# Spreading RMS-norm factors over the partitions: two transposes in place of a matmul with ones

## The chip, the cores and the metric

The kernel runs on one core of a Trainium2 chip. The metric is the device time of one execution in microseconds. The kernel before was timed three times: 938.61, 938.96 and 939.32 us, median 938.96.

## The reference, cut to what matters

The reference is a two-layer streaming encoder on 256 tokens of 1024 features, float32. Each layer is a half-step SwiGLU feed-forward block (FFN), a mixer, and a second half-step FFN. The mixer of layer 0 is a recurrent block (causal convolution and a gated linear recurrence), that of layer 1 differential attention with shared keys and values. Every block starts with an RMS norm over the features:

```
y = x * rsqrt(mean(x*x, axis=-1) + 1e-6) * g
FFN:  x = x + 0.5 * ((silu(h @ w_gate) * (h @ w_up)) @ w_down)      h = rmsnorm(x, g), hidden width 2816
```

The factor rsqrt(...) is one number per token. It commutes with the matrix product, so it can be applied to the product in place of the input.

## The kernel before, in words

The residual x stays in SBUF with the features on the partitions: eight tiles x[d] of 128 x 256 (tokens along the free axis). A block's input is g * x, split into a high part and a low part in fp32r; the weights are split in the same way, piece by piece, by ScalarE (whi) and VectorE (wlo) as they arrive in DMAs of 1 MB. A product of an FFN is made of two matmuls for each 128 x 128 weight block (mm2): whi against both parts of the input, 512 columns, and wlo against the high part, 256 columns. Elsewhere it is three matmuls of 256 columns (mm3), and in the projections of the attention three of 512.

In an FFN (ffn) the gate and up products of two f-blocks are interleaved first (FG = 2, 64 matmuls), then come f-blocks 2 to 21 (640 matmuls), then eight down products (352 matmuls; in the last FFN one of the eight goes by mm3). After the opening two f-blocks the factors are asked for (rb_fn), and finish scales each f-block: the two parts of the sum leave PSUM without the factor, and one VectorE product per f-block applies rb to gate and up together.

The factors come from rstd. While a block writes x[d], sumsq adds its squares into acc. rstd then makes two products of acc with a column of ones, tokens on the partitions (each is two instructions in the profile), VectorE scales and shifts them (rv), and GpSimd raises to the power -1/2 (rt, 128 x 2: the factor of token p and of token 128 + p). For the FFNs and the recurrent block the factors are needed along the free axis, the same on every partition: VectorE multiplies the identity by each column of rt into a diagonal matrix (diag), TensorE multiplies ones with it (two instructions in the profile), and ScalarE copies the 128 x 256 result to SBUF (rb). This happens five times: in the four FFNs, numbered 0 to 3 here (names f10, f20, l1, f21), and in the recurrent block (mix0). The attention's norm (mix1) takes rt alone (bcast=False).

The order of the work is not that of the program text. Every operation is recorded with its costs (cost, lines 121 to 165), then Recorder.plan lays out a list schedule: at each step it takes the engine that can start first, and there, among the operations that can start within HOLD = 60 ns of the first one, that with the longest tail of work behind it; the tail of a TensorE operation counts all of TensorE's operations that follow in the program text. HOP = 94 is added between engines. The costs that matter here, in the planner's ns: a transpose 109 with a latency of 220; an fp32r matmul 0.4428 per column + 3.3; an fp32 matmul of one column 222 with a latency of 392, of 256 columns 430; a VectorE addition of 256 columns 335, rv 70 with a latency of 156; the power 640 with a latency of 680. The plan then is emitted in that order, so that on the chip each engine runs a fixed list. All instructions go through one line of the emitting loop, so the profile has them all as L378; they are told apart by the names of their tiles: aux is the PSUM pool of two banks that rstd uses, mm the other six banks, w the scratch tiles (diag among them), xs, b and xk inputs of matmuls.

Of the kernel before, what the change touches and what calls it, by code (L numbers as in the profile page):

```python
# [11 lines left out]
F32 = mybir.dt.float32  # L12
# [3 lines left out]
ALU = mybir.AluOpType  # L16
AX = mybir.AxisListType

P = 128
D = 1024  # L20
KD = 8
T = 256
# [393 lines left out]
def trunk(ctx: ExitStack, tc, plan, xT, wts, vec, rows, eye, out):  # L416
    nc = Recorder(tc.nc)

    def pool(name, bufs, **kw):
        return Pool(nc, ctx.enter_context(tc.tile_pool(name=name, bufs=bufs, **kw)), bufs, plan and plan[1])  # L420
# [7 lines left out]
    psa = pool("psa", AB, space=bass.MemoryType.PSUM)  # L428
# [5 lines left out]
    ident = const.tile([P, P], F32, name="ident")  # L434
    ones = const.tile([P, P], F32, name="ones")
# [112 lines left out]
    def rstd(name, bcast=True):  # L548
        acc = acc_state["t"]
        ps = psa.tile([P, 512], F32, name="aux")  # L550
        for t in range(NT):
            nc.tensor.matmul(out=ps[:, t:t + 1], lhsT=acc[:, t * P:(t + 1) * P], rhs=ones[:, 0:1],
                             start=True, stop=True)
        v = wk.tile([P, NT], F32, name="rv")
        nc.vector.tensor_scalar(v, ps[:, 0:NT], 1.0 / D, EPS, op0=ALU.mult, op1=ALU.add)
        rt = const.tile([P, NT], F32, name=f"rt_{name}")
        nc.gpsimd.tensor_tensor(out=rt, in0=v, in1=mhalf[:, 0:NT], op=ALU.pow)
        if not bcast:
            return rt, None
        diag = w1()  # L560
        for t in range(NT):
            nc.vector.tensor_scalar(diag[:, t * P:(t + 1) * P], ident, rt[:, t:t + 1], None, op0=ALU.mult)
        pb = psa.tile([P, 512], F32, name="aux")
        nc.tensor.matmul(out=pb[:, 0:T], lhsT=ones, rhs=diag, start=True, stop=True)
        rb = wk.tile([P, T], F32, name="rb")
        nc.scalar.copy(out=rb, in_=pb[:, 0:T])
        return rt, rb
# [10 lines left out]
    def w1(shape=(P, T), dt=F32):  # L578
        return wk.tile(list(shape), dt, name="w1", bufs=10)
# [170 lines left out]

    xs_mix = new_xs()
    ffn(0, xs, lambda: rstd("f10"), prep(xs_mix, V_MIX[0]), small)

    def recurrent(xs, rb_fn, after):
# [102 lines left out]

    xs_f20 = new_xs()
    recurrent(xs_mix, lambda: rstd("mix0"), prep(xs_f20, V_F2[0]))

    xs_f11 = new_xs()
# [3 lines left out]
    def after_l0(d):  # L865
        pr1(d)
        split_scaled(xkv[d], x[d], vt[:, V_KV + d:V_KV + d + 1])

    ffn(1, xs_f20, lambda: rstd("f20"), after_l0)

    kvrt = {}
# [287 lines left out]
```

## Time and profile before

| | |
|---|---|
| median of three runs | 938.96 us |
| the profiled execution | 939.56 us |
| its span, first to last instruction | 937.5 us |
| outside the span | 2.06 us |
| granted TensorE clock | 0.999 of full speed |
| DMA queue that loads the weights | 51.8% of 16 engines |

The engines in the rows are PE (TensorE's matmuls), PEld (its weight loads), DVE (VectorE), ACT (ScalarE), POOL (GpSimd). A row of the timeline or of a group reads out<-in: for a matmul the moving operand comes first, then the stationary one. A matmul's record runs until its result is written, so the records of successive matmuls overlap; what one costs is the distance from its start to that of the next. The chain of waits is followed back from the last instruction, so a stretch on PE in it means that nothing else held PE up there.

### The profile page before, as it was taken

The page shows a single profiled execution, that of the slowest core. Times are in us where ns is not written, and L with a number is a line of the kernel's source. Part 1 is how long each engine was busy: PE and PEld are TensorE (multiplying, and loading weights), DVE is VectorE, ACT ScalarE, POOL GpSimd, SP SyncE. Part 2 cuts the span into 40 slices and gives each one's busy share as a digit, 9 for nine tenths or more (in the row PEclk, how much of TensorE's full clock was granted, in tenths as well). Part 3 has the DMA queues.
Part 4 walks back from the last instruction along what each step waited for, and adds up shares of the span by engine and source line. Part 5 has one row for each costly group of instructions (what it writes and reads, how often), then busy time and mean ns, then how long its engine had stood idle before and what let it go on. Part 6 is the DMA issues. An engine that isn't in the chain of part 4 may idle for free.

```text
span 937.5 us, 14663 instructions
## 1 busy us (share of the span) xinstructions
PE 930.3 (99%) x5586; PEld 823.8 (88%) x5586; DVE 723.0 (77%) x1226; ACT 579.0 (62%) x1039; POOL 31.1 (3%) x42
## 2 busy tenths in 40 slices
PE   8999999999999999999999999999999999999998
PEld 6888888899998888888888888888878988888887
DVE  7898777679898878867688887666987688888651
ACT  7665565559976565655556566554589866565541
POOL 0210000000000000000000000001230000000000
PEclk9999999999999999999999999999999999999999
DMA  8755555553365555555545555555443545555540
GB/s 310 255 184 196 195 184 197 198 189 135 136 225 186 204 194 180 182 200 200 182 180 182 195 202 185 181 189 191 159 138 133 180 172 187 180 186 203 203 157 17
DMA packets 25990, 172.31 MB, mean 184 GB/s; under 512 B 3136, under 2 KB 4288, under 8 KB 5568
## 3 DMA queue, kind: packets, MB, share of 16 engines
q1 hardware_dynamic: 25920, 171.39, 51.8%
q8 instruction: 43, 0.70, 0.3%
q14 instruction: 27, 0.22, 0.1%
HBM read 170.33 MB, written 1.05 MB: 183 GB/s over the span
## 4 chain that ended last, share of the span: by engine, by line
PE 94%; DVE 3%; POOL 1%; DMA 1%; issue 0%; ACT 0%; SPq 0%; ACTq 0%
PE mm L378 92%; PE aux L378 2%; DVE w L378 1%; DVE wlo L378 1%; DMA xa<-xT 1%; DVE ss L378 0%; POOL facq L378 0%; POOL fac L378 0%; POOL rt_mix L378 0%; ACT w L378 0%; SPq L378 0%; ACT whi L378 0%; ACT xs L378 0%; DVE fac L378 0%; DVE xa L378 0%
## 5 line engine op out<-in xcount | busy, mean ns | idle before, releaser
L378 PE MATMUL mm<-xs,whi 128*128 128x512 f32 (+1 forms) x1632 | 532.5, 379 | 2.1 <-DVE xs L378 1.2
L378 DVE TENSOR_TENSOR wlo<-raw,whi 128x1024 fp32r<-128x1024 f32 (+1 forms) x321 | 390.9, 1220 | 130.5 <-ACT whi L378 129.8
L378 ACT CAST whi<-raw 128x1024 fp32r<-128x1024 f32 (+1 forms) x321 | 335.5, 1048 | 203.2 <-PE mm L378 184.1
L378 PE MATMUL mm<-xs,wlo 128*128 128x256 f32 x1520 | 425.9, 281 | 0.1
L378 PEld LDWEIGHTS mm<-xs,whi 128*128 128x128 f32 x1632 | 298.4, 188 | 62.5 <-DVE xs L378 1.5
L378 PE MATMUL mm<-b,whi 128*128 128x512 f32 (+1 forms) x982 | 293.4, 360 | 0.0
L378 PEld LDWEIGHTS mm<-xs,wlo 128*128 128x128 f32 x1520 | 287.1, 189 | 0.8 <-DVE wlo L378 0.5
L378 PE MATMUL mm<-b,wlo 128*128 128x256 f32 x832 | 233.2, 281 | 0.0
L378 PEld LDWEIGHTS mm<-b,whi 128*128 128x128 f32 x982 | 174.8, 189 | 29.6 <-issue 0.3
L378 PEld LDWEIGHTS mm<-b,wlo 128*128 128x128 f32 x832 | 157.5, 189 | 0.0
L378 ACT ACTIVATE w<-mm 128x256 f32<-128x256 f32 x207 | 79.5, 385 | 117.2 <-PE mm L378 112.4
L378 DVE TENSOR_TENSOR w<-mm,w 128x256 f32<-128x256 f32 x176 | 73.5, 421 | 28.4 <-ACT w L378 27.9
L378 DVE TENSOR_TENSOR w<-w,rb 128x512 f32<-128x512 f32 x88 | 60.1, 686 | 0.4
L378 DVE TENSOR_TENSOR w<-w,w 128x256 f32<-128x256 f32 (+2 forms) x104 | 45.2, 439 | 0.3 <-ACT w L378 0.3
L378 PE MATMUL mm<-whi,xk 128*128 128x512 f32 x128 | 41.2, 396 | 0.0
L378 ACT ACTIVATE w<-w 128x256 f32<-128x256 f32 x88 | 36.4, 417 | 2.4 <-DVE w L378 2.2
L378 DVE TENSOR_TENSOR b<-w,b 128x256 fp32r<-128x256 f32 x88 | 36.4, 416 | 1.9 <-ACT b L378 1.9
L378 ACT CAST b<-w 128x256 fp32r<-128x256 f32 x88 | 35.4, 406 | 2.9 <-DVE w L378 2.8
L378 DVE SCALAR_TENSOR_TENSOR xa<-mm,xa 128x256 f32<-128x256 f32 x32 | 13.5, 423 | 27.1 <-PE mm L378 18.9
L378 PEld LDWEIGHTS mm<-whi,xk 128*128 128x128 f32 x128 | 23.8, 188 | 4.6
L378 PE MATMUL mm<-wlo,xk 128*128 128x512 f32 x64 | 25.1, 393 | 0.0
L378 ACT ACTIVATE xs<-xa,vt 128x256 fp32r<-128x256 f32 x40 | 19.5, 502 | 7.3 <-DVE xa L378 7.3
(124 smaller groups left out, 485.3 us busy)
## 6 DMA issues: line engine op xcount, KB each, us to landing
raw<-wts SPq DMA_DIRECT2D x159, 1024.0 KB, 4.8
raw<-wts SPq DMA_DIRECT2D x3, 512.0 KB, 7.5
outT<-xa SPq DMA_DIRECT2D x8, 128.0 KB, 2.0
xa<-xT SPq DMA_DIRECT2D x3, 256.0 KB, 6.6
raw<-wts SPq DMA_DIRECT2D x2, 256.0 KB, 4.4
rw<-rows SPq DMA_DIRECT2D x1, 320.0 KB, 5.0
xa<-xT SPq DMA_DIRECT2D x1, 260.0 KB, 3.8
ident<-eye SPq DMA_DIRECT2D x1, 64.0 KB, 9.2
```

Source lines behind the costliest of these rows:

```text
L378: getattr(getattr(self.nc, op.eng), op.fn)(*op.a, **op.k)
```

## The change

The two scalings of the identity and the product with ones go. In their place are two transposes on TensorE. Each takes one column of rt, read with a step of zero so that the 128 x 1 column stands for a 128 x 128 matrix with equal columns; its transpose has the factors along the free axis on every partition. The copy to rb is the same. The planner runs anew on the changed list of operations.

```diff
         nc.gpsimd.tensor_tensor(out=rt, in0=v, in1=mhalf[:, 0:NT], op=ALU.pow)
         if not bcast:
             return rt, None
-        diag = w1()
+        pb = psa.tile([P, 512], F32, name="aux")
         for t in range(NT):
-            nc.vector.tensor_scalar(diag[:, t * P:(t + 1) * P], ident, rt[:, t:t + 1], None, op0=ALU.mult)
-        pb = psa.tile([P, 512], F32, name="aux")
-        nc.tensor.matmul(out=pb[:, 0:T], lhsT=ones, rhs=diag, start=True, stop=True)
+            nc.tensor.transpose(pb[:, t * P:(t + 1) * P], rt[:, t:t + 1].broadcast_to([P, P]), ident)
         rb = wk.tile([P, T], F32, name="rb")
         nc.scalar.copy(out=rb, in_=pb[:, 0:T])
         return rt, rb
```

## Rows read from the trace of the kernel before

**Rows 1.** The page: engine, busy us, share of the span, instructions.

```profile
PE 930.3 (99%) x5586; PEld 823.8 (88%) x5586; DVE 723.0 (77%) x1226; ACT 579.0 (62%) x1039; POOL 31.1 (3%) x42
```

**Rows 2.** Chain of waits in order of time: start us, us, what, instructions.

```profile
11.55 7.80 PE mm L378 x44
...
19.69 3.65 PE mm L378 x20
...
283.11 2.81 PE mm L378 x15
285.92 0.43 PE aux L378 x2
286.35 180.39 PE mm L378 x1041
...
712.69 0.87 PE aux L378 x8
...
764.48 169.59 PE mm L378 x999
```

**Rows 3.** Windows: stretch, us; busy us (x instructions) by engine; clock, DMA, GB/s.

```profile
40.00:180.00 140.00, 140.00 (x794) 121.44 (x793) 112.27 (x196) 83.15 (x142) 2.52 (x2) 1.00 0.55 190
300.00:440.00 140.00, 140.00 (x809) 123.44 (x809) 107.73 (x166) 83.22 (x144) 0.00 (x0) 1.00 0.55 192
480.00:620.00 140.00, 140.00 (x810) 123.44 (x810) 107.89 (x165) 82.28 (x142) 0.00 (x0) 1.00 0.53 188
640.00:761.00 121.00, 120.47 (x735) 104.61 (x733) 98.66 (x211) 89.79 (x206) 20.05 (x13) 1.00 0.43 151
770.00:910.00 140.00, 140.00 (x810) 123.44 (x809) 105.74 (x162) 79.46 (x135) 0.00 (x0) 1.00 0.55 192
```

**Rows 4.** Timeline of PE, FFN 1 and FFN 3: start us, us, instruction.

```profile
284.12 0.40 PE L378 MATMUL mm<-xs,whi 128*128 128x512 f32 x1
...
285.18 0.40 PE L378 MATMUL mm<-xs,whi 128*128 128x512 f32 x1
...
286.31 0.39 PE L378 MATMUL mm<-xs,whi 128*128 128x512 f32 x1
...
287.35 0.39 PE L378 MATMUL mm<-xs,whi 128*128 128x512 f32 x1
...
762.25 0.40 PE L378 MATMUL mm<-xs,whi 128*128 128x512 f32 x1
...
763.31 0.40 PE L378 MATMUL mm<-xs,whi 128*128 128x512 f32 x1
```

**Rows 5.** Groups of instructions: busy us, mean ns of one; idle before, releasers.

```profile
L378 PE MATMUL aux<-w,ones 128*128 128x256 f32 x10 | 3.0, 386 | 0.1
L378 PE MATMUL aux<-ident,w 128*128 128x128 f32 x72 | 12.5, 274 | 0.5 <-DVE w L378 0.5
L378 PEld LDWEIGHTS aux<-ident,w 128*128 128x128 f32 x72 | 8.9, 141 | 2.4 <-PE mm L378 0.7 <-issue 0.4 <-ACT b L378 0.2
L378 PEld LDWEIGHTS aux<-w,ones 128*128 128x128 f32 x10 | 1.7, 188 | 0.5 <-PE mm L378 0.4
L378 DVE TENSOR_SCALAR w<-ident,rt_f 128x128 f32<-128x128 f32 x6 | 1.4, 280 | 0.0
```

**Rows 6.** Timeline around the factors of FFN 0 (from 22.78) and FFN 1.

```profile
22.78 0.48 DVE L378 TENSOR_SCALAR w<-ident,rt_f 128x128 f32<-128x128 f32 x2
23.05 0.28 PE L378 MATMUL mm<-xs,wlo 128*128 128x256 f32 x1
23.38 0.30 PEld L378 LDWEIGHTS aux<-w,ones 128*128 128x128 f32 x2 [0.38 <-PE mm L378]
...
24.15 0.28 PE L378 MATMUL mm<-xs,wlo 128*128 128x256 f32 x1
...
283.49 0.70 POOL L378 TENSOR_TENSOR rt_f<-rv,mhalf 128x2 f32<-128x2 f32 x1 [81.83 <-DVE rv L378]
```

## The prediction

> **What bounds the kernel now.** I read the page's table of busy times first: TensorE's matmuls cover 99% of the span, VectorE 77% [rows 1]. A share that high can still hide waits, so the chain of waits in order of time came next. From 24 us to the last matmul it is made of long stretches of matmuls, one per feed-forward block (FFN), with the norm's few aux instructions between them [rows 2]. TensorE's order of work is the bound: what shortens its list shortens the kernel, and what is saved on another engine is worth nothing unless TensorE was waiting for it.
>
> The second thing to see is that TensorE's list does not always run at one pace. In an FFN each weight block gives a whi matmul of 512 columns and a wlo matmul of 256. Two stretches of 140 us, both pure pairs of this kind at a granted clock of 1.00, hold 794 matmuls in the first FFN and 809 in the second [rows 3]. Per matmul that is 140/794 = 176.3 ns and 140/809 = 173.1 ns, 3.2 to 3.4 ns apart; I use 3.3. The timeline around the second FFN's broadcast shows where the pace changes. Three pairs before it take 285.18 - 284.12 = 1.06 us, three pairs after it 287.35 - 286.31 = 1.04 us [rows 4]. No engine is waited for in either. I call them the long and the short rhythm. FFN 0 runs long from end to end. FFN 1 enters long and turns short at the broadcast. FFN 2 is short (810 [rows 3]). FFN 3 enters long (763.31 - 762.25 = 1.06 us for three pairs, just ahead of its broadcast [rows 4]) and is short behind it (810 [rows 3]). The position differs too: in FFN 1 to 3 fifteen matmuls lie between the sum's products and the broadcast [rows 2], so it stands between a whi and its wlo; in FFN 0 it stands after all 64 matmuls of the opening groups (44, then 20 after the sum [rows 2]), between a wlo and the next whi, and there the rhythm stayed long.
>
> **The change, part by part.** The broadcast happens five times: in the four FFNs and in the recurrent block (the attention's norm asks for no broadcast).
>
> *Removed on TensorE:* the product of ones with the diagonal, two instructions each time, ten in all [rows 5]. The chain gives the pair 0.43 us [rows 2] (one of four such is shown). In FFN 0 it costs more: from the wlo at 23.05 to the wlo at 24.15 is 1.10 us [rows 6] where a long pair needs 1.06 / 3 = 0.35 [rows 4], so 0.75. The extra 0.3 is a wait: VectorE's two scalings end at 22.78 + 0.48 = 23.26 and the load of the diagonal begins at 23.38 [rows 6]. Sum removed: 4 x 0.43 + 0.75 = 2.47 us.
>
> *Added on TensorE:* two transposes each time, ten in all. The trace has 72 transposes of the same size with the same identity, all in the attention [rows 5]. In the chain a run of eight takes 0.87 us [rows 2], 0.109 each, so two cost 0.22 us. Sum added: 5 x 0.22 = 1.10 us. The net is 2.47 - 1.10 = 1.37 us less.
>
> The record of one transpose is 274 ns long [rows 5], and it would be a mistake to add those up, because the next instruction begins long before the record ends. [...] The clock, for its part, was 1.00 over the whole stretch that holds the 72 [rows 3].
>
> *The stationary operand with a step of zero* is not in the trace. The load of a transpose's data with unit step takes 141 ns [rows 5], other loads 188 [rows 5], both hidden behind the matmul before. I take the 141 as nearest. If the zero step made it the 188, 47 ns each could show: 10 x 0.047 = 0.5 us lost; if it were faster, nothing is won, since the load is hidden.
>
> *The new wait.* The transposes wait on GpSimd's power directly, and every later matmul queues behind them on TensorE. Where do they stand? The order is the planner's, from its own costs (lines 121 to 165). From the first of the sum's two products it counts 222 + 392 + 94 to the earliest start of rv, some 15 more because VectorE is in an addition, 156 + 94 to the power, 680 + 94 to TensorE: 1747. TensorE in that plan has 444 for the two products and then whi and wlo by turns, 230 and 116.7: after three pairs and a whi it stands at 1714, and 1747 lies within HOLD's 60. So in FFN 1 to 3 the transposes come after the seventh matmul, again between a whi and its wlo, eight matmuls earlier than the broadcast now. In FFN 0 the 64 opening matmuls go first and the place stays. In the recurrent block, made of triples of 256 columns, they land inside a triple; the trace shows no second pace there to lose. On the chip the power of FFN 1 ends at 283.49 + 0.70 = 284.19 [rows 6]; the seventh matmul is the whi of 284.12 [rows 4], and the slot after it comes 0.23 later, at 284.35. The hop seen from VectorE to TensorE is 0.12 [rows 6], so the load begins near 284.31. It fits, or slips by up to 0.1 us. Five such slips are 0.5 us, the upper bound; I take none, since a queue that loads ahead has most of the 0.1 covered.
>
> *Removed on VectorE:* ten scalings of 280 ns [rows 5], 2.8 us, at nothing, since VectorE is at 77%. *Earlier:* rb by about 1.3 us (VectorE's queue and the scalings drop out). In the FFNs the sums leave PSUM before rb is needed, so TensorE gains nothing from it. *Moved:* no DMA; a w1 buffer becomes free, and the aux bank is taken by the same two claims. The new plan also reorders ScalarE's and VectorE's lists a little behind each broadcast; at 77% and less they cover it, and I price it at nothing.
>
> Sum: the profiled execution took 939.56 us, its span 937.5. Less 1.37 it is 938.19. The median of the runs is 938.96, 0.60 below that execution, and I carry the same 1.37 over: **937.6**. With the bounds (0.5 lost in loads, 0.5 in slips, or 0.55 more won if half of the transposes' time is hidden) and 0.35 for the spread of the runs, its own range is 936.7 to 938.95. A change of 0.2% (1.9 us) is about what a measurement can tell from none, so this case is mostly "the same".
>
> **The rivals.**
>
> *A, slower: an FFN loses the short rhythm.* The place is the re-entry after the inserted instructions in FFN 1, 2 and 3; it decides if the stream comes out of two transposes in the long rhythm. The matmuls behind the insertion are 1041 in FFN 1 (the opening of FFN 2 among them) [rows 2], 977 in FFN 2 (the same less 64) and, of the 999 in FFN 3 [rows 2], 933 that are pairs. At 3.3 ns that is 3.4, 3.2 and 3.1 us; one lost gives 937.6 + 3.2 = 940.8, two 944.1, all three 947.3. For it: the stream enters FFN 0, 1 and 3 in the long rhythm by itself, only the broadcast was seen to break it, and transposes leave a different spacing behind them than 0.43 us of matmul. Against it: the place between whi and wlo is kept, and there both streams that came in long went out short, the third stayed short.
>
> *B, faster: FFN 0 also turns short.* Its 992 matmuls behind the broadcast would save 3.3 us: 934.3. For it: a stall of 0.3 us goes and the re-entry is another. Against: between wlo and whi no insertion in the trace changed the rhythm, neither the broadcast nor the sum's products.
>
> *C: the change is no gain.* Each transpose costs its record's 274 ns after all [rows 5], ten of them 2.74 us against the 2.47 removed: 0.3 over, 939.2. For it: the load with step zero is unseen. Against it: 0.109 in the chain. [...]
>
> **How the numbers follow.** Forecast 0.36. A 0.46, with one FFN 0.14, two 0.12, three 0.20: two sightings of the turn, of one instruction alone, are thin evidence that transposes do it too. B 0.10, C 0.08. The likeliest single case sets the time, 937.6, and its own range stands above. The range for all runs from the forecast's low end to A in full, with the same spread: 936.7 to 947.7, leaving out B. Faster by over 0.2%: B and 0.05 of the forecast, 0.15. Slower: two and three FFNs, and half of one (it lies on the line), 0.39. The same: the rest, 0.46.
>
> **What would show it.** In the chain, the aux pairs at the five places at 0.22 instead of 0.43 (0.75 in FFN 0), with seven matmuls ahead of them in FFN 1 to 3. In windows of 140 us, 809 matmuls in FFN 1, 2 and 3 and 794 in FFN 0 make the forecast right; 794 in one of the three is A, 809 in FFN 0 is B. VectorE's busy time falls by 2.8 us without effect. The forecast's reasons are wrong if TensorE's load shows a wait for the power of more than 0.1 us, or if the pace differs in stretches that the change does not touch.

## The result: 944.93 us, 0.6% slower, and the profile after

The kernel after took 944.93 us (median of 6 runs, 944.52 to 946.16) against 939.03 us before (6 runs, 938.61 to 940.37). The ratio is 1.0061, 95% interval [1.0051, 1.0071]. The profiled execution took 945.03 us with a span of 942.7, 5.2 us more than the span before. Forecast were 937.6 us and "the same"; what came is rival A with two FFNs lost (944.1 us).

The page of the kernel after, the line that answers to [rows 1]:

```profile
PE 936.3 (99%) x5586; PEld 823.5 (87%) x5586; DVE 721.6 (77%) x1216; ACT 577.6 (61%) x1039; POOL 32.4 (3%) x42
```

TensorE is still busy 99% of the span, but for 6.0 us longer, with the same 5586 instructions. So no new idle time explains the loss: the same list takes longer. The windows of the kernel after say where (stretch; matmul time and instructions; clock, DMA share, GB/s), against 794, 809, 810 and 810 in [rows 3]:

```profile
40.00:180.00 140.00, 140.00 (x795) 1.00 0.56 191
300.00:440.00 140.00, 140.00 (x809) 1.00 0.55 190
480.00:620.00 140.00, 140.00 (x794) 1.00 0.55 188
770.00:910.00 140.00, 140.00 (x794) 1.00 0.55 187
```

FFN 2 and FFN 3 have gone from the short to the long rhythm. In these windows FFN 0 is long and FFN 1 is short, as before, and the granted clock is 1.00 (the 2.4 GHz level) in all four. The chain of waits of the kernel after (start us, us, what, instructions) shows the five places:

```profile
19.82 2.54 PE mm L378 x14
22.36 0.22 PE aux L378 x2
22.57 177.33 PE mm L378 x1016
...
201.66 0.22 PE aux L378 x2
...
282.45 1.52 PE mm L378 x8
283.97 0.32 PE aux L378 x2
...
467.80 0.22 PE aux L378 x2
...
765.08 0.22 PE aux L378 x2
```

The pair of aux instructions has fallen from 0.43 us [rows 2] to 0.22, in FFN 1 to 0.32. They stand behind 8 matmuls there and behind 14 in FFN 0, not behind 7 and 20.

The window of FFN 0 hides a turn. Its whi matmuls ahead of the transposes and behind them, in the timeline of the kernel after (start us, us, instruction):

```profile
20.81 0.40 PE L378 MATMUL mm<-xs,whi 128*128 128x512 f32 x1
...
21.85 0.39 PE L378 MATMUL mm<-xs,whi 128*128 128x512 f32 x1
...
22.76 0.40 PE L378 MATMUL mm<-xs,whi 128*128 128x512 f32 x1
...
23.82 0.40 PE L378 MATMUL mm<-xs,whi 128*128 128x512 f32 x1
```

Three pairs take 21.85 - 20.81 = 1.04 us ahead and 23.82 - 22.76 = 1.06 us behind: here the stream came in short, and the two transposes left it long. In the kernel before, three pairs of the same opening, between the sum and the product, take 1.06 us (whi at 21.39 and at 22.45), so a stretch ahead of the changed instructions ran at another pace too.

Two more views of the kernel after: first the groups of the transposes and their loads (busy us, mean ns; idle before), then the timeline of FFN 1's first transpose (start us, us).

```profile
L378 PE MATMUL aux<-ident,rt_f 128*128 128x128 f32 x6 | 1.2, 280 | 0.0
L378 PEld LDWEIGHTS aux<-ident,rt_f 128*128 128x128 f32 x6 | 0.7, 134 | 0.3 <-POOL rt_f L378 0.2
```

```profile
283.10 0.70 POOL L378 TENSOR_TENSOR rt_f<-rv,mhalf 128x2 f32<-128x2 f32 x1 [81.89 <-DVE rv L378]
...
283.85 0.19 PEld L378 LDWEIGHTS aux<-ident,rt_f 128*128 128x128 f32 x2 [0.20 <-POOL rt_f L378]
```

The load with a step of zero takes 134 ns and is hidden like the 141 of [rows 5]. In FFN 1 it waited for the power, which ended at 283.10 + 0.70 = 283.80, 0.05 us ahead of it. That is the 0.1 us between 0.32 and 0.22.

Cut at the first of each norm's two sum products (the last stage ends with the start of the last matmul), the two timelines give these stages in us:

| stage | before | after | difference |
|---|---|---|---|
| FFN 0 to the recurrent norm | 181.00 | 180.42 | -0.6 |
| recurrent norm to FFN 1 | 82.43 | 82.21 | -0.2 |
| FFN 1 | 183.97 | 183.84 | -0.1 |
| FFN 2 to the attention's norm | 207.33 | 210.38 | +3.1 |
| attention to FFN 3 | 86.83 | 86.89 | +0.1 |
| FFN 3 | 173.03 | 175.94 | +2.9 |

The prediction's saving is in the first three rows, term by term: it forecast 0.75 - 0.22 = 0.53 us for FFN 0 and 0.21 for each of the next two, and the third lacks the 0.1 of the wait. Two lost rhythms are in the fourth row and the last.

### The profile page after: what moved, and what is told of

It reads as the page before. It is cut to its first block, busy times and chain, and to the rows that moved or that the text cites. A ratio compares the mean times of both kernels' runs of the same rounds, so it can differ in the third digit from the quotient of the medians.

```text
span 942.7 us, 14653 instructions
## 1 busy us (share of the span) xinstructions
PE 936.3 (99%) x5586; PEld 823.5 (87%) x5586; DVE 721.6 (77%) x1216; ACT 577.6 (61%) x1039; POOL 32.4 (3%) x42
## 3 DMA queue, kind: packets, MB, share of 16 engines
HBM read 170.33 MB, written 1.05 MB: 182 GB/s over the span
## 4 chain that ended last, share of the span: by engine, by line
PE 95%; DVE 3%; POOL 1%; issue 0%; DMA 0%; ACT 0%; SPq 0%; ACTq 0%
PE mm L378 92%; PE aux L378 2%; DVE w L378 1%; DVE wlo L378 1%; DMA xa<-xT 0%; DVE ss L378 0%; POOL facq L378 0%; POOL fac L378 0%; POOL rt_mix L378 0%; ACT w L378 0%; DVE fac L378 0%; ACT xs L378 0%; DVE xs L378 0%; DVE xa L378 0%; SPq L378 0%
## 5 line engine op out<-in xcount | busy, mean ns | idle before, releaser
L378 PE MATMUL mm<-xs,whi 128*128 128x512 f32 (+1 forms) x1632 | 538.0, 383 | 1.4 <-DVE xs L378 1.4
```

Of the source, the lines that this page charges most:

```text
L378: getattr(getattr(self.nc, op.eng), op.fn)(*op.a, **op.k)
```

## The experiments

The question was what sends an FFN into one rhythm or the other: the place of the inserted instructions (between a whi and its wlo, or between a wlo and the next whi), the instructions themselves, or the moment at which the stream is entered again. For every run I counted the matmuls in the same four windows of 140 us; 809 or 810 is short, 794 or 795 long. All of them together, in the order in which they are told (the kernel before, run alongside, had medians of 938.8 to 939.0 us):

| run | inserted in FFN 1 to 3 | windows of the profiled execution | median us | ratio to before |
|---|---|---|---|---|
| after | whi wlo, 2 transposes, whi; after 8 | 795 809 794 794 | 944.93 | 1.0061 [1.0051, 1.0071] |
| e1_seven | whi, 2 transposes, wlo; after 7 | 810 810 809 810 | 941.67 | 1.0014 [0.9989, 1.0039] |
| e2_lohi | wlo, product with ones, whi; after 16 | 810 810 810 809 | 936.41 | 0.9971 [0.9960, 0.9981] |
| e3_late | whi, 2 transposes, wlo; after 15 | 795 810 794 810 | 941.43 | 1.0019 [1.0008, 1.0031] |
| e4_hhll | as after; grouped whi whi wlo wlo | 806 806 806 806 | 937.73 | 0.9989 [0.9979, 0.9998] |
| e5_hhll_before | product; grouped by two | 806 806 806 806 | 938.65 | 0.9998 [0.9988, 1.0007] |
| e6_h4l4 | 2 transposes; grouped by four | 801 801 801 801 | 942.15 | 1.0038 [1.0023, 1.0053] |
| e7_only3 | as before; as after in FFN 3 | 810 809 810 794 | 938.83 | 1.0002 [0.9993, 1.0012] |
| e8_three | wlo, 3 transposes, whi; after 8 | 795 794 795 794 | 948.27 | 1.0099 [1.0084, 1.0114] |
| e9_sixteen | wlo, 2 transposes, whi; after 16 | 795 794 794 794 | 947.48 | 1.0086 [1.0061, 1.0111] |
| e10_six | wlo, 2 transposes, whi; after 6 | 794 809 809 794 | 944.94 | 1.0045 [1.0026, 1.0064] |
| e11_four | wlo, 4 transposes, whi; after 16 | 809 809 809 810 | 935.66 | 0.9967 [0.9954, 0.9980] |
| e12_apart | one transpose after 14, one after 16 | 810 809 809 810 | 934.83 | 0.9958 [0.9941, 0.9975] |

**e1_seven: the place forecast.** In the emitted order, the wlo ahead of the transposes goes behind them.

```diff
+            if t.fn == "transpose" and "rt_" in t.a[1].tensor.name and lo.fn == hi.fn == "matmul":
+                if (width(hi.k["rhs"]), width(lo.k["rhs"])) == (2 * T, T):
+                    seq.remove(lo.i)
+                    seq.insert(seq.index(pe[p + 1].i) + 1, lo.i)
```

> The changed kernel, with one wlo matmul moved from before the two transposes to behind them in each of the four FFNs, so that the transposes stand between a whi and its wlo (after 13 matmuls in FFN 0, after 7 in FFN 1 to 3). Theory of the rhythm, place decides: all four FFNs run short behind the transposes, 807 to 810 matmuls in each window of 140 us; against the changed kernel (944.9) FFN 2, 3 and 0 each save 3.1 to 3.3 us: 935.2. Theory of the rhythm, fine timing decides: any mixture, 3.2 us for each FFN with 794 in its window, and the total follows that count: 935.2 plus 3.2 for each long one. Rival without rhythm (the transposes, or the earlier rb, or the new order of VectorE and ScalarE cost the time): no change, 944.9.

The ten runs lie in steps: two at 934.8 and 934.9, one at 937.6, five from 941.5 to 942.4, two at 944.6 and 945.1. The profiled execution, 934.8 us, has all four windows short. That the higher steps are one, two and three long FFNs is an inference from their distances of 2.7 to 4.2 us; only the fastest was profiled. So the place between whi and wlo can leave all four short, and does not hold them there.

**e2_lohi: the product in the other kind of place.** The kernel before, with the product moved one wlo later.

```diff
+            if all(q.fn == "matmul" for q in (hi, b, lo)) and "ones" in b.k["lhsT"].tensor.name:
+                if (width(hi.k["rhs"]), width(lo.k["rhs"])) == (2 * T, T) and lo.k["rhs"].dtype == F32R:
+                    seq.remove(b.i)
+                    seq.insert(seq.index(lo.i) + 1, b.i)
```

> The kernel before, with its broadcast matmul moved one matmul later in FFN 1 to 3, behind the wlo, so that it stands between a wlo and the next whi as in FFN 0; nothing else changes. Place decides: FFN 1, 2 and 3 stay long as they came in, 794 in each window, 939.0 + 9.7 = 948.7. Fine timing decides: 939.0 plus 3.2 for each FFN of 1 to 3 that shows 794. Rival without rhythm: 939.0, since every instruction of the kernel before is still there, one step apart.

936.41 us (8 runs, 935.67 to 936.82), faster than before. The windows (same columns as above):

```profile
40.00:180.00 140.00, 140.00 (x810) 1.00 0.57 196
300.00:440.00 140.00, 140.00 (x810) 1.00 0.54 190
480.00:620.00 140.00, 140.00 (x810) 1.00 0.55 192
770.00:910.00 140.00, 140.00 (x809) 1.00 0.54 186
```

Even FFN 0 is short, in which nothing was moved. A place between wlo and whi does not by itself mean the long rhythm: the theory of the place falls.

**e3_late: the transposes behind 15 matmuls**, between whi and wlo, where the product stood before. The planner counts 1250 ns more for the power's latency.

```diff
-            return 300 + 170 * n, 340 + 170 * n
+            return 300 + 170 * n, 340 + 170 * n + (1250 if n == NT else 0)
```

> The changed kernel, with 1250 added to the planner's latency of the norm's power, so that the transposes stand where the broadcast matmul stood (after 15 matmuls, between whi and wlo, in FFN 1 to 3; after 21, between whi and wlo, in FFN 0) and rb comes as late as before. Place decides: all four short, 935.2. Fine timing decides: 935.2 plus 3.2 for each long FFN. Rival that the early rb costs the time: 937.6 with the pace of each FFN left as in the changed kernel, which the windows would contradict or bear out.

941.43 us (938.18 to 942.61). The profiled execution (941.11 us) has FFN 0 and FFN 2 long, FFN 1 and FFN 3 short. The same two transposes in the same kind of slot went both ways in one execution. The two that came out long had come in short (347 ns a pair between the sum and the transposes), the two that came out short had come in long (353). But FFN 2 of e1_seven came in short and stayed short, so the pace on arrival does not settle it alone.

**e4_hhll and e5_hhll_before: no alternation.** The FFN matmuls of both kernels are issued as whi whi wlo wlo.

```diff
-                mm2(pa, ba, xa, ...); mm2(pb, bb, xb, ...)
+        nc.tensor.matmul(out=pa, lhsT=ha, rhs=xa_, ...)
+        nc.tensor.matmul(out=pb_, lhsT=hb, rhs=xb_, ...)
+        nc.tensor.matmul(out=pa[:, 0, :], lhsT=la, rhs=xa_[:, 0, :], ...)
+        nc.tensor.matmul(out=pb_[:, 0, :], lhsT=lb, rhs=xb_[:, 0, :], ...)
```

> The changed kernel, with the FFN's matmuls in groups of four, whi whi wlo wlo, instead of whi wlo whi wlo; same matmuls, same columns, other order of accumulation. If the long rhythm belongs to the alternation of 512 and 256 columns, it is gone: each group costs what two short pairs cost (0.693 us), 808 matmuls in each window of 140 us in all four FFNs, and the total is 944.9 less 9.7 or more: 935.2 or, with the openings of FFN 0, 1 and 3 also short (0.2 us each), 934.6. If the long pace belongs to something that lasts longer than one pair (a state of the engine), two of the four windows still show 794 and the total stays near 944.9.

> The broadcast by a matmul, as in the kernel before, with the FFN matmuls grouped whi whi wlo wlo, as in the run of that grouping with transposes (937.73 us median, 806 matmuls in each window of 140 us). In that grouping no second pace was seen, so the difference of the two kernels is the worth of the transposes alone. Theory (the loss is the rhythm's, and the transposes by themselves save the 1.37 us of the prediction's sum): 806 in all four windows again, and 937.73 + 1.37 = 939.1 us. Rival (the transposes themselves cost the 5.9 us, wherever they stand): this kernel is then faster than its twin, 937.73 - 5.9 = 931.8 us. Rival (this grouping too has a second pace, which the twin happened to miss): one window or more at 794, and 3.2 us more for each.

937.73 us with transposes and 938.65 with the product; 806 in all eight windows. In this grouping there is one pace, a little slower than the short one, and the transposes are 0.92 us ahead of the product, where 1.37 was predicted. Of that, 0.3 was the wait of FFN 0's product, and e5_hhll_before has no such wait (the pair takes 0.43 us on its chain), so 1.05 was to be expected. The two intervals in the table overlap: that the transposes are a gain as such is likely, and its size is rough.

**e6_h4l4: groups of four.** As e4_hhll, four whi and then four wlo.

> The kernel after, with the FFN matmuls in groups of four whi and four wlo. Theory (the grouping by two loses some 1.5 ns a pair against the short rhythm, at its changes of width): half as many changes, half of that loss, about 0.4 us an FFN: 937.73 - 1.5 = 936.2 us, 808 matmuls in each window and one pace in all four. Rival (the loss belongs to each matmul, not to a change of width): 937.7 us and 806. Rival (with four in a group there are two rhythms again): windows that differ from one another by 6 or more.

942.15 us and 801 in every window: slower still, where fewer changes of width should have been faster. The theory of a cost per change of width falls. Alternation one by one, if it stays short, is the fastest order seen.

**e7_only3: the transposes in FFN 3 alone.**

```diff
+        if name in ('f21',):
             ... two transposes
+        else:
             ... scalings and product
```

> The kernel before, with the transposes in FFN 3 alone; the order of TensorE's instructions up to FFN 3's opening is that of before. Theory (an FFN's rhythm is set where its stream is entered again, there and then): windows of the first three FFNs as before (794, 809, 810), and FFN 3 long as in the kernel after, where the transposes stand in the same place (794): 939.04 - 0.2 + 3.0 = 941.8 us; should FFN 3 come out short, 938.8 us. Rival (FFN 3 is long after because of what changed ahead of it): 810 in FFN 3, 938.8 us. Rival (transposes by themselves cost 5.9 / 5 = 1.2 us a place): 940.2 us with 810 in FFN 3.

938.83 us. The windows of the profiled execution (939.39 us):

```profile
40.00:180.00 140.00, 140.00 (x810) 1.00 0.56 196
300.00:440.00 140.00, 140.00 (x809) 1.00 0.55 189
480.00:620.00 140.00, 140.00 (x810) 1.00 0.55 192
770.00:910.00 140.00, 140.00 (x794) 1.00 0.54 187
```

FFN 3 is long, as in the kernel after, with nothing changed ahead of it: what sets its rhythm lies at its own start. FFN 0 came as a surprise: short, with the same TensorE instructions up to and behind its product as before. The timeline of this run around FFN 0's product (start us, us, instruction):

```profile
22.19 0.28 DVE L378 TENSOR_SCALAR w<-ident,rt_f 128x128 f32<-128x128 f32 x1
...
22.69 0.30 PEld L378 LDWEIGHTS aux<-w,ones 128*128 128x128 f32 x2
...
23.59 0.39 PE L378 MATMUL mm<-xs,whi 128*128 128x512 f32 x1
...
24.62 0.39 PE L378 MATMUL mm<-xs,whi 128*128 128x512 f32 x1
```

VectorE ended its scalings at 22.47, ahead of the load, and the load waited for nothing. In [rows 6] the load began at 23.38, after the scalings had ended at 23.26. (That row names the matmul ahead as what it waited for; here a load behind the same matmul began at once, which speaks for the scalings.) Three pairs behind the product now take 24.62 - 23.59 = 1.03 us. Equal instructions, one entered behind a wait and one not, left different rhythms. (The 938.83 is thus one FFN won and another lost; the profiled execution also holds a wait of 1.1 us in FFN 1, told of at the end.)

**e8_three: one transpose more**, `for t in (0, 1, 1)` in the kernel after.

> The kernel after, with the second of the two transposes made twice at each of the five places, so that the stream is entered 0.108 us later. Theory (fine timing at each re-entry sets the rhythm): the third transpose itself costs 5 x 0.108 = 0.54 us, and at least one of the four FFNs changes its rhythm against after (long, short, long, long), so the time is off 945.5 us by a multiple of 3.2 us: 942.3, 939.1 or 935.9 us, or 948.7 us. Rival (the loss is a price of the transposes, 5.9 us for ten): 944.9 + 5 x 0.6 = 947.9 us. Rival (the place after the eighth matmul decides, whatever stands there): the four windows as after (795, 809, 794, 794), 945.5 us.

948.27 us (4 runs, 947.89 to 948.43); 795, 794, 795, 794: FFN 1 changed to long. The time alone does not tell the theory (948.7) from the rival of a price for each transpose (947.9); the window of FFN 1, 794 against 809, does.

**e9_sixteen: the transposes in the slots of e2_lohi.** As e3_late with 1450 in place of 1250.

> The transposes in the slots in which the broadcast by a matmul left all four FFNs short (936.41 us): behind 16 matmuls of the opening in FFN 1 to 3 and behind 22 in FFN 0, each time between a wlo and the next whi. Theory (what is inserted sets the spacing of the first instructions behind it and so the rhythm; two transposes between wlo and whi, entered with no wait, went long in 4 sightings of 4): 794 or 795 in the four windows, 935.0 + 4 x 3.2 = 947.8 us; one FFN that escapes, 944.6. Rival (the slot decides): 809 or 810 in all four, 936.4 - 1.2 = 935.2 us. Rival (each entry is a throw of its own): one to three windows at 794, 938.2 to 944.6 us.

947.48 us, 0.3 from the 947.8 expected. Windows, and the chain in FFN 1:

```profile
40.00:180.00 140.00, 140.00 (x795) 1.00 0.55 191
300.00:440.00 140.00, 140.00 (x794) 1.00 0.54 185
480.00:620.00 140.00, 140.00 (x794) 1.00 0.53 186
770.00:910.00 140.00, 140.00 (x794) 1.00 0.55 190
```

```profile
281.97 2.93 PE mm L378 x16
284.90 0.22 PE aux L378 x2
285.12 15.07 PE mm L378 x85
```

Same slots behind 16 matmuls in FFN 1 to 3 (the same kind of slot in FFN 0, behind 20 and 22), no wait at either: the product, 0.43 us, left all four FFNs short and the two transposes, 0.22 us, all four long. What is inserted decides there, not where, and the kernel with the cheaper insertion is the slower one by 947.48 - 936.41 = 11.1 us. Nor does the rhythm on arrival decide: in both kernels the pairs of the opening, between the sum and the insertion, run at 353 ns each in FFN 1 to 3 and at 347 in FFN 0. All four streams came in alike in the two kernels; the product left short, and the transposes long, what had come in long and what had come in short.

**e10_six: the transposes entered behind a wait**, two matmuls earlier than after.

```diff
+                    for i in (lo.i, hi.i):
+                        seq.remove(i)
+                        seq.insert(seq.index(pe[p + 1].i) + 1, i)
```

> The transposes two matmuls earlier than in the kernel after: behind 6 matmuls in FFN 1 to 3 and behind 12 in FFN 0, again between a wlo and the next whi, so that TensorE reaches them 0.35 us earlier and waits for GpSimd's power (0.1 + 0.35 = 0.45 us in FFN 1, 0 to 0.3 in FFN 2 and 3). Theory (the same two transposes in the same kind of slot leave another rhythm when they are entered behind a wait, as FFN 1 of the kernel after did with a wait of 0.1 us and came out short): FFN 1 to 3 at 809 or 810, FFN 0 at 795 when it has no wait: 935.0 + 3.2 + 0.8 for the waits = 939.0 us. Rival (the waits change nothing but add themselves): 795, 809, 794, 794 as after, 944.9 + 0.8 = 945.7 us. Rival (each entry is a throw of its own): any count of long FFNs, 935.8 us plus 3.2 us for each.

944.94 us, but from 938.28 to 945.96. The profiled execution (941.9 us) has FFN 1 and FFN 2 short, FFN 0 and FFN 3 long, and the load waited for the power in all four (0.3, 0.6, 0.3, 0.3 us). FFN 3 was to be short and is long. Behind a wait, then, the two transposes leave either rhythm; the wait does not make it short.

**e11_four: the insertion made as long as the product.** e9_sixteen with `for t in (0, 0, 1, 1)`.

> The kernel with the transposes behind 16 matmuls (947.48 us, all four FFNs long), with each transpose made twice: the insertion now lasts 0.43 us, as long as the product that left all four short in the same slots. Theory (it is the spacing which transposes leave, 0.108 us from one to the next and some 0.31 us from the first whi to its wlo, and not their total length): still 794 or 795 in all four windows, 947.48 + 10 x 0.108 = 948.6 us. Rival (the total length of the insertion decides): 809 or 810 in all four windows, 936.4 us. Rival (each entry is a throw of its own): a mixture, 935.8 us plus 3.2 for each long FFN.

935.66 us (5 runs, 935.46 to 935.84). My theory expected 948.6, and it falls: ten transposes more make the kernel 11.8 us faster than e9_sixteen. The rival of the total length expected 936.4. Windows and the chain in FFN 1:

```profile
40.00:180.00 140.00, 140.00 (x809) 1.00 0.56 197
300.00:440.00 140.00, 140.00 (x809) 1.00 0.55 190
480.00:620.00 140.00, 140.00 (x809) 1.00 0.56 193
770.00:910.00 140.00, 140.00 (x810) 1.00 0.54 187
```

```profile
282.53 0.44 PE aux L378 x4
```

**e12_apart: the pair taken apart.** e9_sixteen, with the whi and wlo ahead of the pair put between its two transposes.

```diff
+                    for i in (lo.i, hi.i):
+                        seq.remove(i)
+                        seq.insert(seq.index(t.i) + 1, i)
```

> The kernel with the transposes behind 16 matmuls (947.48 us, all four FFNs long), with the pair taken apart: the first transpose stands behind 14 matmuls (20 in FFN 0) and the second behind 16 (22), a whi and a wlo between them. The work is the same, and the two now enter the stream twice by 0.108 us instead of once by 0.216. Theory (the rhythm hangs on the spacing at the last entry, which is another with one transpose than with two or three): at least one of the four windows leaves 794, and the time is 947.5 us less 3.2 us for each: 944.3, 941.1, 937.9 or 934.8 us. Rival (any transposes between a wlo and a whi, entered with no wait, leave the long rhythm): 794 in all four, 947.5 us.

934.83 us (4 runs, 934.34 to 934.99), all four short. This version beats both kernels: 0.42% under the kernel before and 10.1 us under the kernel after, with the very work of the kernel after. Windows and the chain in FFN 1:

```profile
40.00:180.00 140.00, 140.00 (x810) 1.00 0.56 196
300.00:440.00 140.00, 140.00 (x809) 1.00 0.55 193
480.00:620.00 140.00, 140.00 (x809) 1.00 0.55 190
770.00:910.00 140.00, 140.00 (x810) 1.00 0.53 186
```

```profile
281.36 0.11 PE aux L387
281.47 0.35 PE mm L387 x2
281.82 0.11 PE aux L387
```

## Why the prediction was wrong, point by point

- **What bounds the kernel** held. TensorE's list is the bound, it runs at two paces, and the time follows the count of FFNs in the long one. The price of a lost FFN was predicted as 3.1 to 3.4 us. FFN 2 and FFN 3 cost 3.1 and 2.9 us more after, each with some 0.2 of the saving in it; all four long against all four short, in e9_sixteen and e12_apart, is (947.48 - 934.83) / 4 = 3.2 us each.
- **The sum of removed and added instructions**, -1.37 us, held in kind, and its size is bracketed. The first three stages show -0.9 of it. With the rhythm the same on both sides, the transposes gain 0.92 us (e5_hhll_before against e4_hhll) and 936.41 - 934.83 = 1.58 us (e2_lohi against e12_apart, where the placing differs a little). In both pairs FFN 0's product waits for nothing, so 1.05 is the figure to set beside them.
- **Rival C**, a transpose at the price of its record, fell: the records are 280 ns [the group above], and two transposes take 0.22 us of the chain. Ten more of them in e11_four than in e12_apart cost 935.66 - 934.83 = 0.83 us, 0.08 each. The Trainium skill ("TensorE: Matmul & The Clock Gate", Part 4: PE-mode transpose) gives about 275 ns; these runs agree with it as the length of a record and not as the price in a stream of matmuls.
- **The load with a step of zero** was to cost nothing and costs nothing (134 ns, hidden). **The slip** at the new wait was to be 0.1 us at most and is 0.1 us, in FFN 1 alone. **VectorE** was to gain 2.8 us without effect; its busy time fell by 723.0 - 721.6 = 1.4 us, without effect. The sum of ten records was too large for that: records of neighbours overlap (two scalings take 0.48 us together in [rows 6], and 280 ns each).
- **The place failed.** "In FFN 1 to 3 the transposes come after the seventh matmul, again between a whi and its wlo", and "in FFN 0 ... the place stays". They came behind the eighth, and in FFN 0 behind 14 of the opening's matmuls. The hand simulation had the planner's times right: laid out by Recorder.plan, the transposes of FFN 1 could start 1746 ns after the sum's first product, and TensorE is free at 1714. It had the order of the decisions wrong. The planner had held back VectorE's addition, and rv and the power behind it, until TensorE's wlo at 1714 was laid, so the transposes were not yet among its candidates there, and HOLD had nothing to choose.
- **The failed step that decided the result** is the choice that "place between whi and wlo is kept, and there both streams that came in long went out short". It read two sightings of one instruction as a property of a slot. e2_lohi and e9_sixteen, the same slots with two different insertions, show four short and four long; e3_late shows both rhythms behind one kind of insertion in one kind of slot. Nor would the forecast place have saved it: e1_seven has the transposes behind the seventh matmul of FFN 1 to 3, between a whi and its wlo, and its median is 941.67 us, with two runs of ten under 936. The forecast priced the exchange of the insertion at nothing for the rhythm. The runs show that the rhythm behind an insertion hangs on what is inserted, and the change put another insertion into every FFN. One of the prediction's own signs of being wrong came with it, a pace that differs where nothing was changed: the opening of FFN 0, 1.06 us for three pairs before and 1.04 after.
- **The argument against rivals A and B** ("between wlo and whi no insertion in the trace changed the rhythm") failed with it. Of the sightings behind it, FFN 0's product is one in which the wait of 0.3 us counted and not the slot: without the wait the same product left FFN 0 short in e7_only3. The sum's products change the rhythm in other runs, told of below.

What the runs show of insertions between a wlo and the next whi, entered with no wait, in profiled executions:

| inserted | on the chain, us | FFNs that came out short | long |
|---|---|---|---|
| one transpose, a pair, one transpose (e12_apart) | 0.11 and 0.11 | 4 | 0 |
| two transposes (after: 0, 2, 3; e7_only3: 3; e9_sixteen) | 0.22 | 0 | 8 |
| three transposes (e8_three) | 0.33 | 0 | 4 |
| four transposes (e11_four) | 0.44 | 4 | 0 |
| the product (e2_lohi; e7_only3: 0) | 0.43 | 5 | 0 |

No row is mixed, though in every row some streams had come in short and some long. Three of the rows rest on one kernel each, whose four or five runs lie within 0.7 us. The kernel after went slow because it put an insertion of 0.22 us, one of the two lengths that leave the long rhythm, in place of one of 0.43 us. Its FFN 1 escaped; it is the one that was entered behind a wait of 0.1 us.

The table holds for these insertions and is no rule for all. The norm's own two sum products (four instructions, 0.34 us) also stand between a wlo and the next whi, with no wait, and they go either way. In FFN 2 the pairs ahead of them ran at 347 ns in the kernel before, e3_late, e7_only3, e2_lohi, e11_four and e12_apart; behind them they ran at 347 in the first three and at 353 in the last three. The first three had their insertion in FFN 1 between a whi and its wlo, the last three between a wlo and a whi. So the pace ahead is not the whole state that an insertion meets. **What stays open:** why these lengths, what in TensorE holds a rhythm over a thousand matmuls, and why two transposes between a whi and its wlo (e1_seven, e3_late) or behind a wait (e10_six) go either way.

## What to carry to other kernels

Where an engine that is busy 99% of the time runs a long stream of alternating shapes, count its instructions in equal windows before and after: if the count differs at one clock and with no wait, the pace itself has changed, and in these runs a small insertion was enough to change it for the whole stream. Such a change is worth what its instructions cost plus what it does to the pace, and the second term can be the larger (some 1 us against 6 here). When it comes out wrong, try another spacing of the same instructions before giving the change up; here one pair of matmuls between the two transposes, in each FFN and with nothing else changed, was worth 947.48 - 934.83 = 12.65 us.

## What the runs showed of the hardware that was not expected

- Streams of alternating 512- and 256-column fp32r matmuls have two paces at a granted clock of 1.00, 809 and 794 matmuls in 140 us; grouped by two they showed one (806 in all eight windows), by four one that is slower (801 in four).
- Behind the insertion an FFN kept its pace to its end, over some 1000 matmuls, in every profiled execution of the alternating order. The time of one kernel can differ from run to run by steps of the size of an FFN's pace: e1_seven from 934.8 to 945.06 us.
- Doubling the transposes of e9_sixteen, ten instructions more, made the kernel 11.8 us faster.
- GpSimd's power on 128 x 2, 0.70 us in [rows 6], took 1.61 us once, in FFN 1 of the profiled execution of e7_only3, and TensorE's load waited 1.1 us behind the scalings that hung on it.
